# First expert's first weights in four buffers of later outputs, overflow loop ahead of group 3, low-part dispatch by token chunk

## The chip, the cores and the metric

The kernel runs on one core of a Trainium2 chip. The metric is the device time of one execution in microseconds (us); lower is better. Engines in the profile: PE is TensorE's matmuls and PEld its weight loads, DVE is VectorE, ACT is ScalarE, POOL is GpSimd, and SP is the queue of SyncE, on which all large loads are issued.

## The reference

One decoder block on 512 tokens of width 1024 in fp32. Two mixers work on the same normalized input, then a mixture of 32 experts with two experts for each token, then a small embedding term:

```python
u = rms_norm(h)
proj = u @ w_in
h = h + (sigmoid(gate_ssd) * ssd_branch(...) + sigmoid(gate_conv) * conformer_branch(...)) @ w_o
h = h + hier_moe(rms_norm(h))
h = h + (p @ w_ple_proj) * sigmoid(rms_norm(h) @ w_ple_gate)
out = rms_norm(h)

def hier_moe(u, wg, bg, we, be, w_gate, w_up, w_down):
    # top-1 of 4 groups, then the top-2 of its 8 experts, with softmax weights
    ...
    hdn = jax.nn.silu(xb @ w_gate[e]) * (xb @ w_up[e])     # 1024 x 512 each
    return hdn @ w_down[e]                                  # 512 x 1024
```

The weights of the 32 experts are 192 MB and all of them are read.

## The kernel before

The kernel is one stream of **units**. A unit has loads (one tile of weights each) and a function that makes its matmuls. `run(n)` calls `step()` until unit `n`; a step first calls `pump()`, then makes the unit's matmuls, then calls `free` for the pages that the unit has used, and runs the jobs and tasks that are due.

`pump()` (line 270) issues the loads in order on SP, as far as `state["room"]` allows. Room is counted in half pages: a raw load of the mixers (512 KB, tag "raw") takes one, a load of expert weights (1 MB, `wide`, tag "w") takes two. There are 11 pages of 1 MB under tag "w", one of which holds the one-hot matrices, so ten expert loads can be ahead of PE. The jobs `job(XD + 1, free, 2)` and the four of `job(NB - i, free, ...)` raise the room in the last mixer units, so that the first expert loads start before the experts do. All waits are set by the tile framework from the use of the tiles: a load into a page waits for the last matmul that read it.

The stages of the profiled execution: mixers and their output projection to about 530 us, the router and the one-hots to 550, experts to 1031, and the end stage (embedding term, norm, output) to 1102.

Of the experts, 7 **groups** are formed (`GROUPS`), each of one or two **quads** of two or three experts. A quad has four gate/up units (`gu_unit`: tensors eg and eu, the halves kp of the contraction) and two down units (`d_unit`: ed). Each of these units takes one load for each expert of its quad. A token's row is sent to its experts' slots by one-hot matmuls, `disp(gi, kp)`, four for a group and 16 matmuls each: eight with the high part `uh` and eight with the low part `ul`. The outputs `y` of a group's experts lie in the tiles ct, btok, k4 and bt and are brought back to the tokens by eight `combine`s, in group 2 of 4 matmuls each (tiles ct, btok, k, bt against glu). `disp`s of the next group and `combine`s of the last one are **tasks**: they are put between the units when a credit of PE time allows it.

The router's one-hots come last ahead of the experts; group 0's four dispatches are made by hand: all high-part matmuls, then (as `u2_lo` makes the low part, first all chunks c of half n = 0, then of half n = 1) the low-part ones, bank by bank.

An overflow loop, `with tc.For_i(0, n_ext)` (lines 1704 and 1705), serves tokens that do not fit their expert's slots. `n_ext` is read on the chip; with these inputs it is 0 and the loop's body is not run. In before it stands behind `run(NC)`, which is behind all experts and ahead of the end stage; SP has issued seven of the eight w_ple_gate loads of the end stage by then.

Of the kernel before, what the change touches and what calls it, by code (L numbers as in the profile page):

```python
# [19 lines left out]
NT = T // 128  # L20
# [47 lines left out]

_CST = {}
PAGES = 11  # L70
BT = dict(room=8, raw=20, hi=1, page=1.27, mm=3.5, cap=5.0, sp=5, fill=[1.8, 0.9], late=[7, 2])


# [63 lines left out]
def tile_hybrid(ctx: ExitStack, tc: tile.TileContext, x, p, chan, rowv, rows, cst, w_in, w_ssd, w_conf, w_o,  # L137
# [111 lines left out]
    jobs = defaultdict(list)  # L249
    state = {"pairs": 0, "n": 0, "load": 0, "room": 4, "split": 0, "lo": 0, "credit": 0, "top": 0}  # L250

    def load(src, wide):
        loads.append(dict(src=src, wide=wide))
        return loads[-1]

    def unit(src, mms, cost=0.0, plain=False):
        srcs = [] if src is None else src if isinstance(src, list) else [src]
        units.append(dict(lds=[load(s, plain) for s in srcs], mms=mms, cost=cost, plain=plain))
        return len(units) - 1

    def job(n, f, *a):
        jobs[n].append((f, a))
# [4 lines left out]
    def task(early, late, cost, f, *a):  # L267
        tasks.append((early, late, cost, f, a))

    def pump():  # L270
        while state["load"] < len(loads):
            ld = loads[state["load"]]
            if state["room"] <= (1 if ld["wide"] else 0):
                return
            src = ld["src"]()
            if ld["wide"]:
                state["room"] -= 2
                ld["t"] = st([128] + list(src.shape[1:]), F32, "w", PAGES)
            else:
                state["room"] -= 1  # L280
                ld["t"] = page([128] + list(src.shape[1:]), F32, "raw")
            nc.sync.dma_start(ld["t"], src)
            state["load"] += 1

    def free(n):
        state["room"] += n
# [68 lines left out]
    def step():  # L355
        n = state["n"]
        top = state["top"]
        if n < NB:
            while state["split"] <= min(max(n + 2, 2 * n - NB + BT["sp"]), top):
                split()  # L360
        else:
            while state["split"] <= min(top, n + (BT["hi"] if n < NC else 6)) and split_hi():
                split_lo()
        pump()
        u = units[n]
        if u["plain"]:
            ws = [ld["t"] for ld in u["lds"]]
            u["mms"](ws)
            free(2 * len(ws))
        elif u["mms"] is not None:  # L370
            u["mms"](u["wh"], u["wl"])
        after(u)

    def run(upto=None):
        while state["n"] < (len(units) if upto is None else upto):
            step()
# [529 lines left out]
    for c in range(NT):  # L906
        js.extend(chunk(c, f0 + c * TUNE["stride"]))
    XD = math.ceil(max(j[0] for j in js if j[1] in (ssd_diag, ssd_skip)))
    job(XD + 1, free, 2)
    if TUNE["first"]:  # L910
        step_jobs(js)
    for w in seq:
# [146 lines left out]
    job(NO, load_h)  # L1059
    NB = len(units)  # L1060
    for i in range(4, 0, -1):
        job(NB - i, free, 2 if i > 1 else BT["raw"] - BT["room"] - 8)

    def add_h(c, n):
        hv = hh_["h"][:, c, n * 512:(n + 1) * 512]
# [134 lines left out]
    def gu_unit(gi, q, i, kp):  # L1200
        quad = GROUPS[gi][q]

        def mms(ws):
            if kp == 0:
                PG[gi, q, i] = acc()
            for kk in range(4):
# [3 lines left out]
        return unit([lambda b=m[0]: weights((eg, eu)[i], b)[:, 4 * kp:4 * kp + 4, :] for m in quad], mms, BT["mm"],  # L1210
                    True)

    def d_unit(gi, q, fp):
        quad = GROUPS[gi][q]

        def mms(ws):
            if fp == 0:
                PY[gi, q] = [acc2(), acc2()]
            for f in (2 * fp, 2 * fp + 1):
                for n in range(2):  # L1220
                    strips(PY[gi, q][n], HT[gi, q][:, f, :], [w[:, f % 2, n * 512:(n + 1) * 512] for w in ws], quad,
                           f == 0, f == 3)
        return unit([lambda b=m[0]: weights(ed, b)[:, 2 * fp:2 * fp + 2, :] for m in quad], mms, BT["mm"], True)
# [112 lines left out]
        fill_pe(state["n"], room)  # L1336

    combined = NB + 4
    for gi, g in enumerate(GROUPS):
        last = gi == len(GROUPS) - 1  # L1340
        first = len(units)
        if last:
            for n in range(2):
                p_unit(n)
            job(first - 6, free, -2)
            job(first - 5, p_load)
            job(first - 5, free, -2)
            for k in range(2):
                job(first - 3 + k, p_tr, k)
            job(first - 2, free, 2)  # L1350
            job(first - 2, free, -8)
        for q in range(len(g)):
            for kp in range(2):
                for i in range(2):
                    u = gu_unit(gi, q, i, kp)
            job(u - 1, hid_act, gi, q)
            job(u, hid_mul, gi, q)
            job(u, fill_now, BT["fill"][0])
# [16 lines left out]
            continue  # L1375
        for n in range(2):
            for c in range(NT):
                task(u + 1, u + 5, 0.23 * 2 * len(g), combine, gi, c, n)
        combined = u + 5
        o = first + (BT["late"][0] if gi == 0 else BT["late"][1])  # L1380
        for q in range(len(GROUPS[gi + 1])):
            job(o, hot, gi + 1, q)
        for kp in range(4):
            task(o + 1, u, 0.115 * 16, disp, gi + 1, kp)
    for i in range(3):
        unit(None, None)
    NC = len(units)
# [201 lines left out]
    for c in range(NT):  # L1589
        hot_first(c)  # L1590
    for i in range(2 * NT):
        u2_lo(i // NT, i % NT)
    N2 = 2 * NEXP


# [93 lines left out]
    for i, f in enumerate((order0, order4, order1, order2, order3, order5, order6, order7, order8)):  # L1689
        job(NB + (i + 1) // 2, f)  # L1690
    pts = [acc() for _ in range(4)]
    for a in range(2):
        for k in range(4):
            disp_mm(0, k, pts[k], a)
    for k in range(4):
        disp_out(0, k, pts[k])
        if k % 2:
            step()
            step()
    run(NC)  # L1700

    W32 = [128, NEXP]
    ext, ntot, icnt, eidf, pos, gat = (R[n] for n in ("ext", "ntot", "icnt", "eidf", "pos", "gat"))
# [1 line left out]
    with tc.For_i(0, n_ext):  # L1705
# [120 lines left out]
                nc.vector.tensor_add(hv, hv, po)  # L1826
        nc.vector.tensor_scalar(icnt, icnt, 1.0, None, op0=OP.add)
    banks.remove(bank)
    if dbg == "moe":
        for c in range(NT):  # L1830
            nc.sync.dma_start(out[c * 128:(c + 1) * 128, :], h[:, c, :])
        return
# [77 lines left out]
```

## Time and profile before

| | us |
|---|---|
| median of 3 runs | 1103.64 |
| range of the runs | 1099.38 to 1104.58 |
| profiled execution, own time | 1103.84 |
| its span, first to last instruction | 1102.1 |
| PE matmuls busy | 1017.3 (92%) |
| VectorE busy | 561.7 (51%) |
| ScalarE busy | 344.7 (31%) |
| DMA traffic | 255.97 MB, 232 GB/s over the span |

The mean granted clock of TensorE is 0.978 of full speed. PE's share of busy time is an average over stages with different limits: what sets the pace is read stretch by stretch, from the DMA's rate and from what PE waits for. In the names, w is a page of weights, eg, eu and ed are the gate, up and down weights of the experts, cj the dispatched tokens, m the hidden activations, Z the residual stream, acc a bank of PSUM.

### The profile page before, as it was taken

How to read it: one execution, taken by the hardware profiler on the slowest of the kernel's cores; microseconds unless marked ns; L12 is line 12 of the kernel's file. 1: busy time of each engine (PE TensorE's matmuls, PEld its weight loads, DVE VectorE, ACT ScalarE, POOL GpSimd, SP SyncE). 2: the span in 40 equal slices, each digit the busy share in tenths (PEclk: the TensorE clock that was granted, in tenths of full speed). 3: DMA queues.
4: the chain of work that ended last, by engine and by line, in shares of the span. 5: the costliest groups of instructions: out<-in, count | busy, mean ns of one | idle time of the engine just before them, and what ended most of it. 6: DMA issues, size and time to landing. Idle time of an engine off the chain costs nothing. (4 is left out here: it accounts for less than half of the span.)

```text
span 1102.1 us, 15676 instructions
## 1 busy us (share of the span) xinstructions
PE 1017.3 (92%) x6262; PEld 673.0 (61%) x6262; DVE 561.7 (51%) x1004; ACT 344.7 (31%) x646; POOL 14.7 (1%) x32
## 2 busy tenths in 40 slices
PE   5999999999989999999799998989979979889796
PEld 4788889877767877788634453433514415345385
DVE  6689998897889955563721311202103002022365
ACT  5433446766443234432411010100100100121263
POOL 1000000000000000000000000000000000000010
PEclk9999999999999999999899999999999999999899
DMA  9323222201422323356189999999999999998701
GB/s 267 95 70 102 89 78 77 77 1 41 113 77 82 110 77 115 109 195 224 40 350 388 372 387 422 420 421 421 420 421 420 420 421 421 417 401 367 284 2 76
DMA packets 95660, 255.97 MB, mean 232 GB/s; under 512 B 4784, under 2 KB 62144, under 8 KB 71008
## 3 DMA queue, kind: packets, MB, share of 16 engines
q1 hardware_dynamic: 94896, 252.73, 60.6%
q0 software_dynamic: 688, 2.22, 0.7%
q8 instruction: 50, 0.82, 0.3%
q14 instruction: 26, 0.21, 0.1%
HBM read 252.83 MB, written 2.10 MB: 231 GB/s over the span
## 5 line engine op out<-in xcount | busy, mean ns | idle before, releaser
L120 PE MATMUL acc<-uh,w 128*128 128x512 f32 x704 | 231.0, 401 | 1.7 <-DVE w L120 1.6
L120 PE MATMUL acc<-w,cj 128*32 128x512 f32 x1664 | 200.3, 599 | 13.6 <-DMA w<-eu 9.9
L120 PE MATMUL acc<-w,uh 128*128 128x256 f32 (+2 forms) x752 | 161.7, 325 | 0.9 <-DVE w L120 0.9
L120 PEld LDWEIGHTS acc<-uh,w 128*128 128x128 f32 x704 | 132.2, 188 | 32.7 <-DVE w L120 2.6
L120 PE MATMUL acc<-w,m 128*32 128x512 f32 (+1 forms) x960 | 132.3, 595 | 19.2 <-DMA w<-ed 14.5
L120 PEld LDWEIGHTS acc<-w,cj 128*32 128x32 f32 x1664 | 54.4, 110 | 137.4 <-issue 106.6
L120 PE MATMUL acc<-ul,w 128*128 128x512 f32 x352 | 137.2, 390 | 0.0
L120 DVE SCALAR_TENSOR_TENSOR cj<-glu,chan,cj 128x512 f32<-128x512 f32 x180 | 130.8, 747 | 2.2
L120 PEld LDWEIGHTS acc<-w,uh 128*128 128x128 f32 x752 | 118.4, 193 | 21.0 <-issue 10.2
L120 DVE TENSOR_TENSOR w<-w 128x1024 fp32r<-128x1024 f32 x86 | 104.6, 1221 | 43.4 <-ACT w L302 43.2
L120 PE MATMUL acc<-w,ul 128*128 128x256 f32 (+2 forms) x488 | 117.2, 307 | 0.0
L302 ACT CAST w<-w 128x1024 fp32r<-128x1024 f32 x86 | 89.6, 1052 | 67.5 <-PE acc L120 54.4
L120 PE MATMUL acc<-w 128*128 128x512 f32 x384 | 102.0, 404 | 3.1 <-ACT w L302 2.4
L120 PEld LDWEIGHTS acc<-w,m 128*32 128x32 f32 (+1 forms) x960 | 44.5, 127 | 91.2 <-issue 53.1
L120 DVE TENSOR_TENSOR k<-k,acc 128x512 f32<-128x512 f32 x21 | 19.2, 913 | 151.4 <-PE acc L120 151.4
L120 PEld LDWEIGHTS acc<-w 128*128 128x128 f32 x384 | 73.9, 194 | 22.2 <-ACT w L302 2.8
L120 DVE TENSOR_TENSOR Z<-Z,acc 128x512 f32<-128x512 f32 x64 | 43.3, 686 | 85.1 <-PE acc L120 85.1
L120 PEld LDWEIGHTS acc<-w,ul 128*128 128x128 f32 x488 | 77.2, 189 | 5.6
L120 PEld LDWEIGHTS acc<-ul,w 128*128 128x128 f32 x352 | 66.2, 188 | 15.1 <-issue 1.7
L1227 ACT ACTIVATE k<-acc 128x512 f32<-128x512 f32 x13 | 7.8, 597 | 160.9 <-PE acc L120 160.9
L120 DVE SCALAR_TENSOR_TENSOR bt<-glu,chan,bt 128x512 f32<-128x512 f32 x60 | 43.0, 748 | 0.7
L120 DVE SCALAR_TENSOR_TENSOR bt<-acc,gt,k 128x512 fp32r<-128x512 f32 x12 | 9.0, 751 | 66.8 <-ACT k L1311 66.1
(270 smaller groups left out, 885.6 us busy)
## 6 DMA issues: line engine op xcount, KB each, us to landing
w<-eg SPq DMA_DIRECT2D x64, 1024.0 KB, 13.7
w<-eu SPq DMA_DIRECT2D x64, 1024.0 KB, 14.8
w<-ed SPq DMA_DIRECT2D x64, 1024.0 KB, 15.1
w<-w_in SPq DMA_DIRECT2D x52, 512.0 KB, 5.1
w<-w_ssd_out SPq DMA_DIRECT2D x8, 512.0 KB, 5.3
w<-w_conf_out SPq DMA_DIRECT2D x8, 512.0 KB, 4.3
w<-w_o SPq DMA_DIRECT2D x8, 512.0 KB, 4.8
w<-w_ple_gate SPq DMA_DIRECT2D x8, 512.0 KB, 13.3
```

The lines of the kernel that those rows point to most:

```text
L120: return f(*a, **k)
L302: nc.scalar.copy(u["wh"], u["raw"])
L1227: nc.scalar.activation(t, PG.pop((gi, q, 0)), AF.Silu)
```

## The change

There are four parts.

1. The first gate/up unit of group 0 becomes `first_unit`: its two loads of 1 MB become four of 512 KB, and these go to the tiles k4 (two buffers), ct and btok, which else are first written by the experts' outputs. Loads with a tag need no room and give none back.
2. The room that is given ahead of the experts comes later: the job behind the mixer's `ssd` steps goes, and the last of the four jobs gives 6 half pages in place of 4.
3. The overflow loop moves from behind the experts to the place between group 2 and group 3 (`LG = 3`). The eight combines of group 2 are made as jobs on its last down unit, ahead of the loop; the four dispatches of group 3, before tasks inside group 2, come right behind the loop.
4. The low part of the first dispatch is made by token chunk: `u2_lo` makes both halves of a chunk before the next, and the low-part matmuls run over the chunks outside and the eight column blocks inside, so that the four banks are complete together.

The loads on SP where the experts' first weights come, before:

```order
L282 DMA w<-w_o 128x2x512 x8
L282 DMA w<-eg 128x2048 x2
L1025 DMA Z<-x 128x1024 x4
L282 DMA w<-eu 128x2048 x2
L282 DMA w<-eg 128x2048 x2
L282 DMA w<-eu 128x2048 x2
```

and now:

```order
L287 DMA w<-w_o 128x2x512 x8
L287 DMA k_3754<-eg 128x1024
L287 DMA k_3756<-eg 128x1024
L287 DMA ct<-eg 128x1024
L287 DMA btok<-eg 128x1024
L287 DMA w<-eu 128x2048
L1029 DMA Z<-x 128x1024 x4
L287 DMA w<-eu 128x2048
```

The first unit's weights are out of the pages, and 1 MB of eu now stands ahead of the four loads of x.

On SP at the loop's new place, with what each row waits for (DMAHW are the counters of SP's loads, eight in all), now:

```order
L287 DMA w<-eg 128x2048 [waits DMAHW7_49,PE_49]
L287 ISA
L287 DMA w<-eu 128x2048 [waits DMAHW0_49,PE_49]
L1731 TENSOR_LOAD cd [waits DVE_49]
L1731 ISA x2
L1732 COMPARE_AND_BRANCH
L1732 UNCONDITIONAL_BRANCH [waits SP_sequencer_49,DMAHW0_49,DMAHW1_49,DMAHW2_49,DMAHW3_49,DMAHW4_49,DMAHW5_49,DMAHW6_49,DMAHW7_49]
```

These rows stood, in before, behind the loads of the end stage, without the waits:

```order
L282 DMA w<-ed 128x2048
L282 DMA w<-w_ple_gate 128x2x512 x7
L1704 TENSOR_LOAD cd
L1704 ISA x2
L1705 COMPARE_AND_BRANCH
L1705 UNCONDITIONAL_BRANCH x2
```

Seven loads of group 3 stand ahead of the loop on SP, and the eighth behind it.

On PE at the start of group 3, before (w,cj is a gate/up unit of 32 matmuls; ct, btok, k, bt against glu are one combine of group 2):

```order
L120 MATMUL acc<-bt,glu 128x512
L120 MATMUL acc<-w,cj 32x512 x16
L120 MATMUL acc<-ct,glu 128x512
L120 MATMUL acc<-btok,glu 128x512
L120 MATMUL acc<-k_5827,glu 128x512
L120 MATMUL acc<-bt,glu 128x512
L120 MATMUL acc<-ct,glu 128x512
L120 MATMUL acc<-btok,glu 128x512
L120 MATMUL acc<-k_5827,glu 128x512
L120 MATMUL acc<-bt,glu 128x512
L120 MATMUL acc<-w,cj 32x512 x32
L120 MATMUL acc<-w,uh 128x256 x8
```

and now, from the end of the loop (w,uh and w,ul are the two parts of a dispatch):

```order
L1732 REGISTER_ALU
L1732 COMPARE_AND_BRANCH
L1732 UNCONDITIONAL_BRANCH
L122 MATMUL acc<-w,uh 128x256 x8
L122 MATMUL acc<-w,ul 128x256 x8
L122 MATMUL acc<-w,uh 128x256 x8
L122 MATMUL acc<-w,ul 128x256 x8
L122 MATMUL acc<-w,uh 128x256 x8
L122 MATMUL acc<-w,ul 128x256 x8
L122 MATMUL acc<-w,uh 128x256 x8
L122 MATMUL acc<-w,ul 128x256 x8
L122 MATMUL acc<-w,cj 32x512 x64
```

All eight combines of group 2 are ahead of the loop; four dispatches of group 3 follow it, and only then the group's gate/up units, with no other work between them.

The diff:

```diff
--- before.py
+++ after.py
@@ -68,6 +68,8 @@
 
 _CST = {}
 PAGES = 11
+
+LG = 3
 BT = dict(room=8, raw=20, hi=1, page=1.27, mm=3.5, cap=5.0, sp=5, fill=[1.8, 0.9], late=[7, 2])
 
 
@@ -249,13 +251,14 @@
     jobs = defaultdict(list)
     state = {"pairs": 0, "n": 0, "load": 0, "room": 4, "split": 0, "lo": 0, "credit": 0, "top": 0}
 
-    def load(src, wide):
-        loads.append(dict(src=src, wide=wide))
+    def load(src, wide, tag=None):
+        loads.append(dict(src=src, wide=wide, tag=tag))
         return loads[-1]
 
-    def unit(src, mms, cost=0.0, plain=False):
+    def unit(src, mms, cost=0.0, plain=False, tags=None):
         srcs = [] if src is None else src if isinstance(src, list) else [src]
-        units.append(dict(lds=[load(s, plain) for s in srcs], mms=mms, cost=cost, plain=plain))
+        lds = [load(s, plain, t) for s, t in zip(srcs, tags or [None] * len(srcs))]
+        units.append(dict(lds=lds, mms=mms, cost=cost, plain=plain))
         return len(units) - 1
 
     def job(n, f, *a):
@@ -270,10 +273,12 @@
     def pump():
         while state["load"] < len(loads):
             ld = loads[state["load"]]
-            if state["room"] <= (1 if ld["wide"] else 0):
+            if not ld["tag"] and state["room"] <= (1 if ld["wide"] else 0):
                 return
             src = ld["src"]()
-            if ld["wide"]:
+            if ld["tag"]:
+                ld["t"] = st([128] + list(src.shape[1:]), F32, *ld["tag"])
+            elif ld["wide"]:
                 state["room"] -= 2
                 ld["t"] = st([128] + list(src.shape[1:]), F32, "w", PAGES)
             else:
@@ -366,7 +371,7 @@
         if u["plain"]:
             ws = [ld["t"] for ld in u["lds"]]
             u["mms"](ws)
-            free(2 * len(ws))
+            free(sum(2 for ld in u["lds"] if not ld["tag"]))
         elif u["mms"] is not None:
             u["mms"](u["wh"], u["wl"])
         after(u)
@@ -906,7 +911,6 @@
     for c in range(NT):
         js.extend(chunk(c, f0 + c * TUNE["stride"]))
     XD = math.ceil(max(j[0] for j in js if j[1] in (ssd_diag, ssd_skip)))
-    job(XD + 1, free, 2)
     if TUNE["first"]:
         step_jobs(js)
     for w in seq:
@@ -1059,7 +1063,7 @@
     job(NO, load_h)
     NB = len(units)
     for i in range(4, 0, -1):
-        job(NB - i, free, 2 if i > 1 else BT["raw"] - BT["room"] - 8)
+        job(NB - i, free, 2 if i > 1 else BT["raw"] - BT["room"] - 6)
 
     def add_h(c, n):
         hv = hh_["h"][:, c, n * 512:(n + 1) * 512]
@@ -1209,6 +1213,18 @@
                        k == 0, k == KD - 1)
         return unit([lambda b=m[0]: weights((eg, eu)[i], b)[:, 4 * kp:4 * kp + 4, :] for m in quad], mms, BT["mm"],
                     True)
+
+    def first_unit():
+
+        quad = GROUPS[0][0]
+
+        def mms(ws):
+            PG[0, 0, 0] = acc()
+            for k in range(4):
+                strips(PG[0, 0, 0], XT[0, k // 2][:, k % 2, :QS], [ws[2 * e + k // 2][:, k % 2, :] for e in range(2)],
+                       quad, k == 0, False)
+        return unit([lambda b=m[0], i=i: weights(eg, b)[:, 2 * i:2 * i + 2, :] for m in quad for i in range(2)], mms,
+                    BT["mm"], True, [("k4", 2), ("k4", 2), ("ct", 1), ("btok", 1)])
 
     def d_unit(gi, q, fp):
         quad = GROUPS[gi][q]
@@ -1336,9 +1352,12 @@
         fill_pe(state["n"], room)
 
     combined = NB + 4
+    NL = None
     for gi, g in enumerate(GROUPS):
         last = gi == len(GROUPS) - 1
         first = len(units)
+        if gi == LG:
+            NL = first
         if last:
             for n in range(2):
                 p_unit(n)
@@ -1352,7 +1371,7 @@
         for q in range(len(g)):
             for kp in range(2):
                 for i in range(2):
-                    u = gu_unit(gi, q, i, kp)
+                    u = first_unit() if gi == q == i == kp == 0 else gu_unit(gi, q, i, kp)
             job(u - 1, hid_act, gi, q)
             job(u, hid_mul, gi, q)
             job(u, fill_now, BT["fill"][0])
@@ -1375,13 +1394,17 @@
             continue
         for n in range(2):
             for c in range(NT):
+                if gi == LG - 1:
+                    job(u, combine, gi, c, n)
+                    continue
                 task(u + 1, u + 5, 0.23 * 2 * len(g), combine, gi, c, n)
         combined = u + 5
         o = first + (BT["late"][0] if gi == 0 else BT["late"][1])
         for q in range(len(GROUPS[gi + 1])):
             job(o, hot, gi + 1, q)
         for kp in range(4):
-            task(o + 1, u, 0.115 * 16, disp, gi + 1, kp)
+            if gi != LG - 1:
+                task(o + 1, u, 0.115 * 16, disp, gi + 1, kp)
     for i in range(3):
         unit(None, None)
     NC = len(units)
@@ -1589,7 +1612,7 @@
     for c in range(NT):
         hot_first(c)
     for i in range(2 * NT):
-        u2_lo(i // NT, i % NT)
+        u2_lo(i % 2, i // 2)
     N2 = 2 * NEXP
 
 
@@ -1689,15 +1712,19 @@
     for i, f in enumerate((order0, order4, order1, order2, order3, order5, order6, order7, order8)):
         job(NB + (i + 1) // 2, f)
     pts = [acc() for _ in range(4)]
-    for a in range(2):
-        for k in range(4):
-            disp_mm(0, k, pts[k], a)
+    for k in range(4):
+        disp_mm(0, k, pts[k], 0)
+    w = GW[0]
+    for c in range(NT):
+        for k in range(KD):
+            mm(pts[k // 2][:, k % 2 * w:(k % 2 + 1) * w], R["u2l"][:, c, k * 128:(k + 1) * 128], G["oh", 0][:, c, :w],
+               False, c == NT - 1 and k % 2 == 1)
     for k in range(4):
         disp_out(0, k, pts[k])
         if k % 2:
             step()
             step()
-    run(NC)
+    run(NL)
 
     W32 = [128, NEXP]
     ext, ntot, icnt, eidf, pos, gat = (R[n] for n in ("ext", "ntot", "icnt", "eidf", "pos", "gat"))
@@ -1826,6 +1853,9 @@
                 nc.vector.tensor_add(hv, hv, po)
         nc.vector.tensor_scalar(icnt, icnt, 1.0, None, op0=OP.add)
     banks.remove(bank)
+    for kp in range(4):
+        disp(LG, kp)
+    run(NC)
     if dbg == "moe":
         for c in range(NT):
             nc.sync.dma_start(out[c * 128:(c + 1) * 128, :], h[:, c, :])
```

## Rows read from the trace of the kernel before

**Rows 1.** The page, the span in 40 equal slices: the DMA's GB/s.
```profile
GB/s 267 95 70 102 89 78 77 77 1 41 113 77 82 110 77 115 109 195 224 40 350 388 372 387 422 420 421 421 420 421 420 420 421 421 417 401 367 284 2 76
```
**Rows 2.** Windows: busy us (instructions) of each engine in three stretches; columns above.
```profile
core 0: us, PE busy (x) PEld busy (x) DVE busy (x) ACT busy (x) POOL busy (x), PEclk, DMA share, GB/s
553.00:600.00 47.00, 45.04 (x388) 20.09 (x384) 9.39 (x39) 6.56 (x11) 0.00 (x0) 0.96 0.95 377
741.00:780.00 39.00, 35.65 (x250) 15.09 (x251) 9.52 (x16) 3.16 (x6) 0.00 (x0) 0.96 1.01 421
980.00:1000.00 20.00, 20.00 (x114) 11.79 (x110) 4.64 (x5) 7.28 (x12) 0.00 (x0) 0.96 0.82 319
```
**Rows 3.** PE's waits, largest of 533-660 and of 660-1031: total us, times, longest.
```profile
PE acc L120 <- DVE dtx L120: 5.6, 1, 5.6
...
PE acc L120 <- DMA w<-ed: 14.5, 13, 2.3
```
**Rows 4.** Timeline of SP, 525 to 660: start, length, loads issued.
```profile
528.79 25.39 SPq L282 DMA_DIRECT2D w<-ed  x3
...
580.42 4.25 SPq L282 DMA_DIRECT2D w<-ed  x4
```
**Rows 5.** Single loads issued at 580.42, 747.68 and 757.91: KB, us to landing.
```profile
w<-ed SPq DMA_DIRECT2D x1, 1024.0 KB, 5.0
...
w<-eu SPq DMA_DIRECT2D x1, 1024.0 KB, 19.8
...
w<-ed SPq DMA_DIRECT2D x1, 1024.0 KB, 19.4
```
**Rows 6.** Tile Z, 485 to 510: ns of one, first and last start.
```profile
L1025 SPq DMA_DIRECT2D Z<-x x4: 328/422/430, 486.7 to 488.0; - x4
...
L120 DVE TENSOR_TENSOR Z<-Z,acc x4: 687/687/687, 494.4 to 498.6; 128x512 f32<-128x512 f32 x4
```
**Rows 7.** Timelines of PE and of ACT in the router, 538 to 551.
```profile
545.99 3.79 PE L120 MATMUL acc<-w,ul 128*128 128x256 f32 x32
...
547.09 0.59 ACT L1278 COPY cj<-acc 128x512 f32<-128x512 f32 x1 [8.98 <-PE acc L120]
```
**Rows 8.** Timeline around the loop's place in before, 1028 to 1047.
```profile
1040.69 1.22 DVE L120 TENSOR_TENSOR w<-w 128x1024 fp32r<-128x1024 f32 x1
...
1042.42 3.15 PE L120 MATMUL acc<-ident,Z 128*128 128x128 f32 x16 [3.53 <-DVEq L1705]
...
1043.94 0.75 DVE L120 SCALAR_TENSOR_TENSOR ul<-acc,chan,uh 128x512 fp32r<-128x512 f32 x1 [2.03 <-PE acc L120]
...
1045.22 1.20 PE L120 MATMUL acc<-w,uh 128*128 128x512 f32 x2
```
**Rows 9.** Line 1705, the loop: ns min/median/max, first and last start in us.
```profile
L1705 SPq EVENT_SEMAPHORE  x21: 17/28/2061, 1029.3 to 1042.0; - x21
...
L1705 DVEq COMPARE_BRANCH  x3: 41/51/61, 1039.8 to 1043.7; - x3
```
**Rows 10.** Timeline of SP at the boundary of groups 2 and 3, 730 to 786.
```profile
747.68 6.96 SPq L282 DMA_DIRECT2D w<-eu  x2
```
**Rows 11.** Timeline of PE at the same place, 741 to 787.
```profile
750.09 4.56 PE L120 MATMUL acc<-w,m 128*32 128x512 f32 x25 [1.44 <-DMA w<-ed]
...
758.63 0.50 PE L120 MATMUL acc<-ct,glu 128*128 128x512 f32 x1
...
764.40 3.64 PE L120 MATMUL acc<-w,cj 128*32 128x512 f32 x32
...
777.03 1.18 PE L120 MATMUL acc<-w,uh 128*128 128x256 f32 x8
...
778.96 0.60 PE L120 MATMUL acc<-ident,k 128*128 128x128 f32 x4
```
**Rows 12.** Windows, one stretch behind PE's waits of 745 to 750 (columns as in rows 2).
```profile
749.50:752.90 3.40, 2.81 (x16) 0.79 (x20) 0.00 (x0) 0.00 (x0) 0.00 (x0) 0.50 1.02 424
```
**Rows 13.** Timeline of PE, 974 to 1030.
```profile
977.97 5.32 PE L120 MATMUL acc<-w,m 128*32 128x512 f32 x26 [2.29 <-DMA w<-ed]
```

## The prediction

> **What bounds the kernel now.** I read the page's slices first: their GB/s row swings between 1 and 390 until the 25th slice and then stands at 420 nearly to the end [rows 1]. Stretch by stretch the windows say the same: 553 to 600 us has TensorE's matmuls (PE) busy 45 of 47 us at 377 GB/s, so PE sets the pace there; from 741 to 780 the weights arrive at 421 GB/s and PE idles 3.4 of 39 us; from 980 to 1000 PE is busy all 20 us and the DMA falls to 319 GB/s [rows 2]. PE's waits agree. Between 533 and 660 us the largest is 5.6 us for VectorE in the router, and no wait for a load of weights is listed; between 660 and 1031 us its largest item is 14.5 us for ed loads [rows 3]. So from about 650 to 1031 us the stream of weights is the bound, 1 MB (1.049 million bytes at 420 GB/s) in 2.5 us, and what stops that stream for a microsecond costs one.
>
> **First weights.** In before, ten pages hold the first ten loads; the row of three ed issues from 528.79 lasts 25.39 us, since the third waits until the first expert unit gives pages back [rows 4]. With the first two loads in other buffers, the first twelve land before PE has finished a unit. The thirteenth still waits for the second unit's pages, as it does in before. PE waits for no load until after 660 us [rows 3], and at 580.42 one ed load is back in 5.0 us, alone on an empty queue: the DMA had run dry waiting for a page that PE held [rows 4, 5]. The lead is gone by then. I take 0. The bounds are 0 and a gain of two loads, 2 x 2.5 = 5.0 us, if the lead lasted into the stretch that the DMA bounds. The x loads into Z stand behind 1 MB more on SP, 2.5 us; they are issued from 486.7, and VectorE's first addition needs them at 494.4, 7.7 us later [rows 6]; 2.5 + 5.0 us for a load on an empty queue [rows 5] is 7.5. So 0, with 0.5 us at worst. The raw pages that come two later lie in a stretch where loads land tens of microseconds ahead of use: 0.
>
> **Router.** In before the low part is 32 matmuls from 545.99 to 549.7, and the first copy out of PSUM runs at 547.09, when the first quarter is finished, for 0.59 us [rows 7]; the first expert matmul follows the 32nd at once. The new order finishes all four banks only in its last eight matmuls, which begin at 549.7 - 0.9 = 548.8, so the first copy moves to about 549.1, ends at 549.7, and the first expert matmul moves to about 549.9: +0.2 us (0.1 to 0.6, where one copy shows in full).
>
> **The loop at the end, removed.** PE sits idle 3.53 us ahead of its transposes at 1042.42, released by VectorE's sequencer at the loop's line, and VectorE 2.03 us at 1043.94 [rows 8]. Without the loop the transposes follow the last combine directly, but VectorE is at a weight split until 1040.69 + 1.22 = 1041.9, and makes ul (0.75 us) before the first products. These come at 1045.22 now [rows 8]; 1041.9 + 0.75 + 0.1 = 1042.75 then, 2.5 us earlier. Since PE no longer idles ahead of them, its clock may stay up where it would else fall (below): I take -2.9 us (-2.0, VectorE's idle alone, to -3.5, all of PE's).
>
> **The loop in the middle, added.** The order shows what passing it needs: SP waits at the branch for all eight DMA semaphores, and then every engine for all others. Nothing runs through it. (The loop's body runs zero times with these inputs: no load in the trace is issued by its lines.) Its own instructions are cheap, 41 to 61 ns a branch on VectorE, while SP's semaphore waits there go up to 2061 ns [rows 9]. [...]
>
> Step one, the drain. SP has issued seven loads of group 3 when it comes to the loop, the last of them the eu of 747.68, which lands 19.8 us later, at 767.5 [rows 5, 10]. PE's last down unit of group 2 ends at 754.65. Eight combines are 32 matmuls; 24 take 758.63 to 764.40, so 32 take 7.7 us, and with some 2 us for the four outputs ahead of them PE is through by 764.3 [rows 11]. The loads end last. At the end of before 0.4 us lie between the loop's last wait (1042.0) and PE's first matmul [rows 8, 9]: PE restarts at 768.0 and SP issues at about 768.1. A load on an empty queue takes 5.0 us [rows 5], so the next one lands at 773.1 and not, as the stream would have it, at 767.5 + 2.5 = 770.0. The DMA has lost 3.1 us.
>
> Step two, the refill. Of ten pages seven are full, so SP may issue three, the last landing at 778.1. The fourth waits for pages of the group's first unit, and in front of that unit the change has put four dispatches, which before had been done during group 2. One is 16 matmuls, 1.93 us (777.03 to 778.96 [rows 11]), so four are 7.7 us. [...] A unit takes 3.6 us (764.40 to 768.0 [rows 11]). 768.0 + 7.7 + 1.7 + 3.6 = 781.0, and 5.0 later, at 786.0, the fourth load is there. In before it is an ed begun at 757.9 that takes 19.4 us, 777.3 [rows 5]. The stream is now 8.7 us late: 7.0 if the clock holds, 9.4 if the first unit too sees half of it.
>
> Step three. Units two to four give eight pages back in all by 791.8, eight loads that last to 786.0 + 7 x 2.5 = 803.5. The ninth needs a down unit, and four dispatches of group 4, which had stood between units, now stand ahead of it: 791.8 + 7.7 + 3.6 + 0.7 (transposes) = 803.8, and 5.0 to land is 808.8, against 806.0 in a stream without a gap. 2.8 us more (1.5 to 3.5). From there a quad's four units give pages faster than the DMA fills them. Sum 11.5 us (8.5 to 12.9).
>
> All of it reaches the end: PE waits for ed in before at 977.97 for 2.29 us [rows 13], after which it has no slack that could take it back; the PE-bound stretch from 980 moves along as a whole.
>
> [...]
>
> **Sum.** The profiled execution took 1103.84 us (span 1102.1), 0.2 above the median of 1103.64. 1103.84 + 0 + 0.2 - 2.9 + 11.5 = 1112.6 us.
>
> **Rivals.** *Only the drain counts*: the stream loses 3.1 us at the loop, but the dispatches behind it cost the DMA nothing, because more pages are free than I count or PE gets further ahead while group 2 lacks dispatches. 1103.84 + 0.2 - 2.9 + 3.1 = 1104.2. For it speaks that PE has 14.5 us of waits for ed loads alone to spend after 660 [rows 3]; against it that ten pages hold 25 us of stream, and PE alone gives them back. *The loop is nearly free*, by the mechanism that SP's wait ends with loads already queued behind it: 1103.84 + 0.2 - 2.9 = 1101.1. Against it stand the order's waits for every DMA semaphore. *Faster*: this, and the first weights' lead of 5.0 us lasts: 1096.1. It decides from the point where PE waits for a load within the first two groups, and the rows show none. *The dear loop*, on my own side: passing it costs 2 us more on each engine since VectorE's last branch there came only at 1043.7, 1.7 us behind SP's last wait at 1042.0 [rows 9]; were that so on PE and SP in the new place, it would give 1114.6 and, with the upper end of each step, 1117.
>
> **How the numbers follow.** A measurement of this kernel tells some 0.5%, 5.5 us, from no change. My forecast, with its own range of 1109 to 1116, gets 0.58 and the dear loop 0.07, both slower by over 0.5% (from 1109.2). Only the drain: 0.17; the nearly free loop: 0.07; both within. Faster: 0.11. The range reaches down to the free loop and up to the dear one, 1100 to 1117. Slower 0.64, same 0.25, faster 0.11.
>
> **What would show it.** In the profile after, the DMA's windows should show a gap of about 3 us near 768, a second of 5 to 6 us near 780 and a third near 806, at 420 GB/s between them; PE idle from about 764 to 768 and at 0.5 granted behind it; no PE wait for loads before 660; first products of the end stage 2.5 us closer to the last combine. Wrong would be a stream that runs through 768 without a gap, a queue that is full again before 780, or first experts' units that start earlier than 549.

## The result and the profile after

The changed kernel takes 1109.03 us (median of 5 runs, 1108.62 to 1111.48). Runs of the kernel before beside it bring that one to 1102.14 us (5 runs, 1099.38 to 1104.58). The ratio is 1.007 with a 95% interval of 1.0052 to 1.0088: slower by 0.7%, or 6.9 us. The profiled execution of the changed kernel took 1109.03 us, its span is 1107.3 us, 5.2 us longer than the span of before; the profiled execution of before lay 1.7 us above its median.

The page has the loss in one row, the DMA's GB/s in 40 slices, to be laid beside [rows 1]:

```profile
GB/s 266 99 70 106 79 85 69 77 1 55 98 58 96 78 113 114 164 246 199 31 381 396 369 405 421 421 421 302 318 408 421 421 421 420 415 419 376 331 1 76
```

Three slices behind the 27th, at 302, 318 and 408, had been at 420. The windows of 10 us from 760 on (us, busy us of each engine, PE's granted clock, DMA share, GB/s) cut this finer:

```profile
760.00:770.00 10.00, 4.97 (x23) 4.97 (x24) 1.50 (x5) 0.59 (x1) 0.00 (x0) 0.66 0.47 161
770.00:780.00 10.00, 10.00 (x95) 6.28 (x97) 0.00 (x0) 1.76 (x3) 0.00 (x0) 1.00 0.54 190
780.00:790.00 10.00, 10.00 (x95) 3.78 (x88) 1.09 (x1) 0.60 (x1) 0.00 (x0) 1.00 0.98 408
790.00:800.00 10.00, 10.00 (x91) 7.43 (x89) 0.00 (x0) 2.83 (x5) 0.00 (x0) 1.00 1.00 416
800.00:810.00 10.00, 10.00 (x92) 4.83 (x92) 2.65 (x10) 2.44 (x4) 0.00 (x0) 1.00 0.87 330
810.00:820.00 10.00, 8.76 (x74) 2.32 (x66) 0.00 (x0) 0.60 (x1) 0.00 (x0) 1.00 0.98 393
```

At 420 GB/s the six would add up to 2520, and they add up to 1898. The stream of weights lost 622 x 10 / 420 = 14.8 us. In 741 to 780 of before it had lost none [rows 2].

PE's timeline around the loop, columns as in [rows 11]:

```profile
745.68 5.32 PE L122 MATMUL acc<-w,m 128*32 128x512 f32 x26 [1.45 <-DMA w<-ed]
750.92 0.50 PE L122 MATMUL acc<-ct,glu 128*128 128x512 f32 x1
...
758.34 0.40 PE L122 MATMUL acc<-bt,glu 128*128 128x512 f32 x1
765.03 2.08 PE L122 MATMUL acc<-w,uh 128*128 128x256 f32 x8 [6.29 <-issue]
...
774.76 13.94 PE L122 MATMUL acc<-w,cj 128*32 128x512 f32 x128
788.64 1.21 PE L122 MATMUL acc<-w,uh 128*128 128x256 f32 x8
...
796.62 3.64 PE L122 MATMUL acc<-w,m 128*32 128x512 f32 x32
```

and SP's, with single loads from the narrow windows at 743.26, 764.76 and 778.43 below it (us to landing last):

```profile
743.26 21.84 SPq L287 DMA_DIRECT2D w<-eu  x2
765.32 13.97 SPq L287 DMA_DIRECT2D w<-ed  x4
781.87 3.77 SPq L287 DMA_DIRECT2D w<-eg  x3
...
800.29 5.35 SPq L287 DMA_DIRECT2D w<-eg  x3
```
```profile
w<-eu SPq DMA_DIRECT2D x1, 1024.0 KB, 19.7
...
w<-eu SPq DMA_DIRECT2D x1, 1024.0 KB, 5.0
...
w<-ed SPq DMA_DIRECT2D x1, 1024.0 KB, 5.0
```

This is the picture that was forecast. The seventh load, of 743.26, lands at 763.0; PE is idle for 6.3 us; SP issues again at 764.76, and the lone load lands 5.0 us later, at 769.8. PE then makes four dispatches, until 774.7, and a first unit. The load that waits for the unit's pages goes out at 778.43 and lands at 783.4. Four dispatches of group 4 stand between the units and the down unit of 796.62, and SP, which has issued a load at 789.30, issues none until 800.29.

What was not forecast stands in the first rows. The last down unit of group 2 ends at 751.0, not at 754.65 [rows 11], and the seventh load lands at 763.0, not at 767.5 [rows 5]. The changed kernel came to the loop 4.5 us early. Most of this arises in the mixers. The largest of PE's waits between 300 and 535 us (total us, times, longest), before and after:

```profile
PE acc L120 <- ACT k L929: 2.9, 1, 2.9
```
```profile
PE acc L122 <- DVE dtx L122: 5.6, 1, 5.6
PE acc L122 <- DVE w L122: 3.1, 3, 1.6
```

(The dtx wait is the router's; it is in both, at 538.42 before and at 533.61 after, and only the window's end keeps it out of the first list.) The 2.9 us for the squares of the LayerNorm (line 929) is gone after. Before, it stands at 413.78, and the stretch behind it ran at a granted clock of 0.51 (414.90 to 418.40), while the same work ran at 1.00 after:

```profile
413.78 1.05 PE L120 MATMUL acc<-ones,k 128*128 128x1 f32 x8 [2.93 <-ACT k L929]
```
```profile
414.90:418.40 3.50, 3.50 (x9) 2.72 (x9) 1.62 (x2) 1.11 (x2) 0.00 (x0) 0.51 0.00 0
```
```profile
410.50:415.00 4.50, 4.50 (x30) 4.01 (x30) 0.00 (x0) 1.12 (x2) 0.00 (x0) 1.00 0.73 233
```

2.9 us and half of 3.5 make 4.7, and the router's wait comes 4.8 us earlier, 533.61 in place of 538.42.

At the end the changed kernel goes straight on, with nothing between combine and transposes. PE's last wait for weights before, and then the same wait and PE's first products after, to be compared with [rows 8]:

```profile
1029.17 5.32 PE L120 MATMUL acc<-w,m 128*32 128x512 f32 x26 [1.52 <-DMA w<-ed]
```
```profile
1038.25 3.62 PE L122 MATMUL acc<-w,m 128*32 128x512 f32 x26 [1.47 <-DMA w<-ed]
...
1046.18 1.91 PE L122 MATMUL acc<-ident,Z 128*128 128x128 f32 x16
...
1047.84 0.47 PE L122 MATMUL acc<-w,uh 128*128 128x512 f32 x1
...
1049.36 0.50 PE L122 MATMUL acc<-w,uh 128*128 128x512 f32 x1 [1.04 <-DVE w L122]
...
1051.81 0.50 PE L122 MATMUL acc<-w,ul 128*128 128x512 f32 x1 [0.83 <-DVE ul L122]
```

PE's last wait for an ed load is at 1029.17 before and at 1038.25 after, 9.1 us later. The transposes are 3.8 us later than before, the first products 2.6, and after the waits for VectorE's splits the span ends 5.2 us later: 3.9 us come back at the end. Not all of this is the loop's: 1.7 us are the last down unit, whose 26 matmuls take 5.32 us at a mean granted clock of 0.67 before (1029.2 to 1034.4) and 3.62 us at 1.00 after (1038.3 to 1041.8). (They take 5.16 us in a run below that has no loop at all, so it is not the loop's absence behind them that makes them short.) That leaves 2.2 us. The account of the two traces is then -4.5 (mixers, as the stream sees it) + 14.8 (loop) - 1.2 (given back by the stream between 820 us and its end) - 3.9 (end) = 5.2 us. The 1.2 is what remains, not a row; it fits that from 980 to 1000, where PE was busy throughout in before, its stream ran at 319 GB/s [rows 2] and that of the changed kernel at 410: the late stream caught up there.

### The profile page after: what moved, and what is told of

Same layout as the page of the kernel before. It is cut to its first block, busy times and chain, and to the rows that moved or that the text cites. A ratio compares the mean times of both kernels' runs of the same rounds, so it can differ in the third digit from the quotient of the medians.

```text
span 1107.3 us, 15680 instructions
## 1 busy us (share of the span) xinstructions
PE 1012.1 (91%) x6262; PEld 670.6 (61%) x6262; DVE 561.3 (51%) x1004; ACT 344.7 (31%) x646; POOL 14.5 (1%) x32
## 5 line engine op out<-in xcount | busy, mean ns | idle before, releaser
L122 PE MATMUL acc<-w,cj 128*32 128x512 f32 x1632 | 194.4, 594 | 16.3 <-DMA w<-eu 10.4
L122 PE MATMUL acc<-w,m 128*32 128x512 f32 (+1 forms) x960 | 128.3, 574 | 23.7 <-DMA w<-ed 18.4
## 6 DMA issues: line engine op xcount, KB each, us to landing
w<-ed SPq DMA_DIRECT2D x64, 1024.0 KB, 14.3
```

Of the source, the lines that this page charges most:

```text
L122: return f(*a, **k)
```

## The experiments

Three theories stood after this. A: the later raw pages gave the mixers their 4.7 us, and the moved loop costs far more than the drain that one sees. B: the terms of the prediction as put. C: the first weights' lead made the 4 us.

**The four parts apart.** The loop moved alone (part 3 of the diff, nothing else of it):

```diff
...
-    run(NC)
+    run(NL)
...
+    for kp in range(4):
+        disp(LG, kp)
+    run(NC)
```

> Before with the loop move alone (part 3: loop, eight combines ahead of it, four dispatches of group 3 behind it). Theory A (the later raw pages gave the mixers 4.7 us, the moved loop costs the weight stream 14.5 us and gives 3.9 back at the end): mixers as in before, first expert matmul at 549.7, the stream some 14 to 15 us later behind the loop, the whole 10 to 11 us slower than before. Theory B (the prediction as put: the later raw pages are worth nothing, the loop costs 11.5 and gives 2.9): 8.6 us slower, as 1112 us. Theory C (the first weights' lead made the whole 4 us): as A.

Measured: 1115.04 us beside 1101.86 of before, ratio 1.0129 (1.0095 to 1.0162), 13 us slower. The mixers are as in before (first expert matmul at 548.4, the 2.9 us wait is there). The profiled span is 1111.2 us, 9.1 above that of before; the other three runs were slower than the profiled one. By the interval the move costs 10.5 to 17.9 us: A's 10 to 11 reaches its lower end, and B's 8.6 is too little.

Parts 1, 2 and 4 without part 3:

```diff
...
-    run(NL)
+    run(NC)
...
```

> The changed kernel with the loop, the combines and the dispatches of group 3 back in their old places (parts 1, 2 and 4 alone). Theory A: first expert matmul near 545.6 and 4 us faster than before, near 1099. Theory B: 0.2 us slower than before. Theory C: 4 us faster, but with the mixers' end where it was and the lead arising in group 0.

Measured: 1098.65 us, ratio 0.9964 (0.9947 to 0.9981), 3.2 us by the medians. A and C hold, B falls. Part 2 alone tells them apart:

```diff
-    job(XD + 1, free, 2)
...
-        job(NB - i, free, 2 if i > 1 else BT["raw"] - BT["room"] - 8)
+        job(NB - i, free, 2 if i > 1 else BT["raw"] - BT["room"] - 6)
```

> Before with the room given later alone (part 2: two half pages not at the mixer's ssd steps but with the last raise). Theory A: PE's wait of 2.9 us for the LayerNorm squares near 414 is gone with its half-clock stretch, first expert matmul at 545.0, 4.7 us faster than before. Theories B and C: PE's waits as in before, no change (within 0.5 us).

Measured: 1098.48 us, ratio 0.9961 (0.9945 to 0.9977), on the same chip as the run above. PE's wait of 2.9 us is gone, and the first expert matmul is at 545.72. Part 2 alone gives all that parts 1, 2 and 4 give together, so the first weights' four buffers are worth nothing that can be measured. (Part 1 alone, with the room of before, was not run.) C falls. And part 4:

```diff
-        u2_lo(i // NT, i % NT)
+        u2_lo(i % 2, i // 2)
...
-    for a in range(2):
-        for k in range(4):
-            disp_mm(0, k, pts[k], a)
+    for k in range(4):
+        disp_mm(0, k, pts[k], 0)
+    w = GW[0]
+    for c in range(NT):
+        for k in range(KD):
+            mm(pts[k // 2][:, k % 2 * w:(k % 2 + 1) * w], R["u2l"][:, c, k * 128:(k + 1) * 128], G["oh", 0][:, c, :w],
+               False, c == NT - 1 and k % 2 == 1)
```

> Before with the low-part dispatch by token chunk alone (part 4). Theory A, from the two traces: first expert matmul 0.6 us later than in before, 550.3. Theory B, from the prediction: 0.2 us later, 549.9. Either way no change that the time can tell.

Measured: 1101.61 us, ratio 0.9997 (0.9982 to 1.0013); first expert matmul at 549.28, 9.8 us behind the first high-part matmul, where before has 9.9. Neither theory's shift, of 0.6 or 0.2 us, is seen. The 0.6 to 0.7 us that the two traces show between these points belong to a longer stretch at a granted clock of 0.50, from 535.0 to 541 after and from 539.8 to 544 before (the high part takes 6.99 us after and 6.36 before, and 7.07 in the run of part 2 alone), not to the order.

**Why half pages given later help.** In the order (the instructions of an engine with what each waits for, as shown under the change), the casts of the mixers' last weights wait in turn for VectorE and for PE in before, and each for both in the changed kernel. That is one reading of the gain. The rival is that the number of half pages counts. One half page in place of two:

```diff
-    job(XD + 1, free, 2)
+    job(XD + 1, free, 1)
...
-        job(NB - i, free, 2 if i > 1 else BT["raw"] - BT["room"] - 8)
+        job(NB - i, free, 2 if i > 1 else BT["raw"] - BT["room"] - 7)
```

> Before with one half page, not two, given later (one at the ssd steps as now, one with the last raise). In the order, the casts of the weights then wait in turn for VectorE and for PE, as in before, and not each for both, as in the changed kernel. Theory A (what counts is which page a cast falls on): PE's wait of 2.9 us near 414 stays and the time does not change (within 1 us). Rival (what counts is how much is given later): half the gain of e3_room_only, 2 us faster.

Measured: 1097.03 us, ratio 0.9941 (0.9917 to 0.9964). Both expectations failed: neither no change nor half the gain, but all of it. So the alternation of the casts as a whole isn't the cause. ScalarE's timeline shows which cast it is; before, and then this run:

```profile
404.41 0.63 ACT L929 ACTIVATE k<-bt 128x512 f32<-128x512 f32 x1 [0.32 <-ACT k L929]
410.10 1.04 ACT L302 CAST w<-w 128x1024 fp32r<-128x1024 f32 x1 [5.06 <-PE acc L120]
413.10 0.63 ACT L929 ACTIVATE k<-cj 128x512 f32<-128x512 f32 x1 [1.95 <-DVE cj L120]
```
```profile
402.86 0.63 ACT L929 ACTIVATE k<-bt 128x512 f32<-128x512 f32 x1 [0.32 <-ACT k L929]
403.40 1.04 ACT L302 CAST w<-w 128x1024 fp32r<-128x1024 f32 x1
406.41 0.63 ACT L929 ACTIVATE k<-cj 128x512 f32<-128x512 f32 x1 [1.97 <-DVE cj L120]
409.90 1.05 ACT L302 CAST w<-w 128x1024 fp32r<-128x1024 f32 x1 [2.85 <-PE acc L120]
```

One cast, of weights that are needed much later, is queued on ScalarE between the squares of the LayerNorm. Its page is the next in the ring of eleven. In before PE was still reading that page, so the cast waited 5.06 us. VectorE's subtraction for the same weights waited for the cast, the LayerNorm's next centred row stood behind the subtraction, and its square, which PE waits for, behind that row. The subtraction, before:

```profile
411.17 1.23 DVE L120 TENSOR_TENSOR w<-w 128x1024 fp32r<-128x1024 f32 x1 [7.16 <-ACT w L302]
```

With one or two half pages of raw weights fewer in flight the same cast finds a page that is free, and in the order it has lost its wait for PE:

```
L302 CAST w<-w 128x1024 [waits DMAHW7_49,PE_49]
```
```
L302 CAST w<-w 128x1024 [waits DMAHW7_49]
```

The first is before, the second this run; the run of part 2 alone has the second too. The casts of this run still wait in turn, as in before, but shifted by one: the cast between the squares is without a wait for PE, and the next one has it (2.85 us at 409.90), where PE loses nothing by it. The chain of waits is read from the traces; no run moved this cast alone. By the ratio, the kernel with one half page is the fastest of all that were run, faster than both kernels of the study. Against part 2 alone (0.9961) its interval overlaps, and which of the two is better stays open.

**The price of the loop at its old place.** Before without the loop:

```diff
-    n_ext = nc.values_load(ntot, min_val=0, max_val=T * 2 // SL + NEXP)
-    with tc.For_i(0, n_ext):
...
-    banks.remove(bank)
```

> Before without the overflow loop at all (left out: what would serve overflowing tokens, none with these inputs). It prices the loop at the end. Theory A (the changed kernel's stretch from the last load to the end): 3.9 us faster than before. Theory B (the prediction's term): 2.9 us faster. Rival: VectorE's work behind the combines hides the loop, under 1 us.

Measured: 1101.72 us beside 1102.32, ratio 0.9988 (0.9970 to 1.0005): A's 3.9 us falls, and B's 2.9 us, the rival's under 1 us and no change at all lie within the interval. The profiled span is 2.0 us shorter. The first products of the end stage come at 1040.20 and not at 1045.22 [rows 8], 5.0 us earlier, and 3.0 us of that are lost again:

```profile
1040.20 0.48 PE L120 MATMUL acc<-w,uh 128*128 128x512 f32 x1
...
1041.77 0.50 PE L120 MATMUL acc<-w,uh 128*128 128x512 f32 x1 [1.09 <-DVE w L120]
...
1044.23 0.50 PE L120 MATMUL acc<-w,ul 128*128 128x512 f32 x1 [0.83 <-DVE ul L120]
```

VectorE splits weights and makes ul for the same products. While PE stood at the loop, VectorE ran ahead; without the loop PE waits for it.

**What the moved loop costs, taken apart.** The changed kernel without the loop, with its order of combines and dispatches:

> The changed kernel without the overflow loop, with its PE order kept (eight combines of group 2, then four dispatches of group 3 ahead of its first unit; left out: the loop). Theory A (drain and order each cost; worked out by the prediction's steps two and three without the drain): PE is through the dispatches by 766 and the first unit by 770, so the stream loses about 2 us there and 3 us at group 4's dispatches, 5 of the 14.5; with 4.4 us from the mixers and 3.9 from the end the whole is near 1099, 3 us faster than before. Theory D (the drain alone is the price, the order is free): no gap of the stream near 770 to 810, 8 us faster than before. Theory O (the order is the price): the stream still loses 9 us, 1 us slower than before.

Measured: 1099.54 us, ratio 0.9968 (0.9949 to 0.9986), where A had 1099. D's 8 us faster and O's 1 us slower lie outside the interval. The windows of the same stretch:

```profile
760.00:770.00 10.00, 10.00 (x94) 5.57 (x96) 0.00 (x0) 1.76 (x3) 0.00 (x0) 1.00 0.87 334
770.00:780.00 10.00, 10.00 (x93) 4.49 (x85) 1.10 (x1) 0.82 (x2) 0.00 (x0) 1.00 1.01 424
780.00:790.00 10.00, 10.00 (x90) 7.24 (x88) 0.00 (x0) 2.77 (x6) 0.00 (x0) 1.00 0.92 380
790.00:800.00 10.00, 10.00 (x94) 4.32 (x98) 2.65 (x10) 2.28 (x4) 0.00 (x0) 1.00 0.98 375
800.00:810.00 10.00, 8.56 (x78) 2.40 (x74) 0.00 (x0) 0.60 (x1) 0.00 (x0) 1.00 1.01 401
```

At 420 GB/s the five would add up to 2100; they are short of it by 186, which is 4.4 us of stream, where A had 5. The order alone costs a third of 14.8 us, the loop with this order the rest.

The drain alone: before with a second loop at the same place, its body one instruction, and combines and dispatches as they were:

```diff
...
+    run(NL)
...
+    with tc.For_i(0, n_ext0):
+        nc.vector.memset(icnt0, 0.0)
     run(NC)
```

> Before with a second loop between groups 2 and 3, whose body is one instruction of VectorE and runs zero times; combines and dispatches stay as in before. It prices the drain alone. Theory A: the stream loses 4 to 5.5 us (the first lone load and the one behind it) and then runs on, as the first unit follows the loop at once: 4 to 5.5 us slower than before. Theory D (the drain with what it does to the pages is the whole price): 14 us slower. Theory F (passing a loop is nearly free): under 1 us.

Measured: 1111.86 us, ratio 1.0076 (1.0053 to 1.0100), 8.4 us slower by the ratio. A fell here: the drain without any dispatch behind it is not a matter of 4 to 5.5 us. D's 14 us is outside as well. PE's timeline shows what A had left out:

```profile
751.75 3.62 PE L120 MATMUL acc<-w,m 128*32 128x512 f32 x26 [1.44 <-DMA w<-ed]
769.65 5.84 PE L120 MATMUL acc<-w,cj 128*32 128x512 f32 x32 [14.29 <-DMA w<-eu]
...
781.20 3.64 PE L120 MATMUL acc<-w,cj 128*32 128x512 f32 x32
```

PE stands for 14.3 us, since the eight combines that fill 7.8 us of this time in the changed kernel now lie behind the loop, six between the first unit and the second (781.20) and two behind the second. The first unit itself takes 5.84 us in place of 3.64 [rows 11], at a mean granted clock of 0.57 from 769 to 775. The stream restarts (the four ed issues begin at 770.15), and then waits for PE's pages again (the next issues begin at 784.87): its windows from 755 to 821 are short of 420 GB/s by 11.6 us of stream. Together with the 4.4 us of the order alone that is 16.0, and the changed kernel has 14.8, so the two do not simply add up. Of the 11.6 us some 8.4 reach the time.

**Whether each gap counts.** If the stream's gaps were prices of their own, then moving dispatches from ahead of the first unit would pay. Two of the four dispatches behind the second unit:

```diff
-    for kp in range(4):
-        disp(LG, kp)
+    for kp in range(2):
+        disp(LG, kp)
+    for kp in range(2, 4):
+        job(NL + 1, disp, LG, kp)
```

> The changed kernel with two of group 3's four dispatches ahead of its first unit and two behind its second unit. Theory P (what counts is when PE, as a whole behind, gives back the pages of the down unit; the gaps ahead of it only share that delay out): first unit 3.9 us earlier and the second gap of the stream down from 5.2 to 1.5 us, but a new gap behind the second unit, and the stream after 806 as late as in the changed kernel; the time within 1 us of the changed kernel's 7 us over before. Theory G (each gap of the stream counts for itself, as the prediction's steps add them): 3.9 us faster than the changed kernel, 3 us over before.

Measured: 1109.30 us beside 1102.31, ratio 1.0067 (1.0046 to 1.0088): as slow as the changed kernel. Then the same with the planner's credit charged for the four dispatches, so that one dispatch of group 4 fewer stands ahead of the down unit:

```diff
+    state["credit"] -= 0.115 * 16 * 4
```

> e9_split_dispatch with the credit of PE time charged for the four dispatches, so that three and not four of group 4's dispatches stand ahead of group 3's first down unit. Theory P: one dispatch of 1.9 us fewer ahead of the down unit, the stream after 806 us 1.9 us earlier than in e9 and 5 us over before. Theory G: 1.9 us less again, 1 us over before. If the refill has nothing to do with it: no change, 7 us over before in both.

Measured: 1107.83 us, ratio 1.0046 (1.0031 to 1.0061). Both times are as theory P had them; the 95% intervals of the two runs overlap, but all five runs of the second are faster than all four of the first. The windows, of the first and then of the second:

```profile
770.00:780.00 10.00, 10.00 (x90) 4.85 (x89) 0.00 (x0) 0.73 (x2) 0.00 (x0) 1.00 0.86 333
...
790.00:800.00 10.00, 10.00 (x91) 7.36 (x89) 0.00 (x0) 2.83 (x5) 0.00 (x0) 1.00 0.71 297
```
```profile
770.00:780.00 10.00, 10.00 (x92) 5.44 (x88) 0.00 (x0) 1.13 (x2) 0.00 (x0) 1.00 0.96 378
...
790.00:800.00 10.00, 10.00 (x91) 5.56 (x94) 0.62 (x4) 1.76 (x3) 0.00 (x0) 1.00 0.73 279
```

In the first the window of 770 to 780 has gained 143 GB/s over the changed kernel, and the one of 790 to 800 has lost 119; from 760 to 820 its stream is short by 15.1 us, the changed kernel's by 14.8. The loads come earlier, run out earlier, and wait for the same down unit, whose matmuls begin at 796.55, in the changed kernel at 796.62. In the second they begin at 792.53, 4.0 us earlier than in the first, where P had 1.9: the dispatch that is gone makes 1.9 of it, 1.0 is that PE leaves the loop earlier (763.12 for 764.17), and 1.1 that its first two dispatches behind it take 5.4 us (763.12 to 768.50) and not 6.5 (764.17 to 770.66), at a mean granted clock of 0.69 against 0.66 from 760 to 770. So the second run doesn't price the dispatch alone.

## Why the prediction was right, and where it was not

The time (1109.0 for a forecast of 1112.6, at the lower edge of the range of 1109 to 1116) and the side were right, and the reason for the loss too: the stream of weights is drained at the loop, and PE, behind by the dispatches, refills it late. Term by term:

| term | forecast, us | measured, us (from the traces where nothing else is said) |
|---|---|---|
| first weights, x loads | 0 | 0 (parts 1, 2 and 4 beside part 2 alone) |
| later raw pages | 0 | -4.8 |
| router | +0.2 | 0 (its own run) |
| loop in the middle | +11.5 (8.5 to 12.9) | +14.8, of which 1.2 given back |
| loop gone from the end | -2.9 (-2.0 to -3.5) | -3.9 here, 1.7 of it the last down unit's clock; -2.0 where the loop was left out of before |

- **First weights: right.** PE waits for no load before 660 us in the changed kernel either, and parts 1, 2 and 4 together gain no more than part 2 alone.
- **Raw pages: the step that failed.** "The raw pages that come two later lie in a stretch where loads land tens of microseconds ahead of use: 0." The loads were not late. What it left out is that a raw load also takes a place in the ring of pages, so that every later tile of the ring falls on another page with another last reader. One cast between the LayerNorm's squares got rid of its wait, and PE of 2.9 us and a stretch of 3.5 us at 0.51 granted. One of the prediction's own signs of being wrong came with it, first experts' units that start earlier than 549: in the changed kernel the first starts at 545.60. No bound of this term reached below zero in the forecast, and the rivals had no such mechanism. PE's wait at 413.78 could be followed back in the trace of before, over ScalarE, VectorE and the cast, to PE itself.
- **Router: right in effect.** The later first copy is not seen in the time.
- **The loop in the middle: mechanism right, size short by 3.3 us.** The drain was put at 3.1; from the landing at 763.0 to the next at 769.8 it is 6.8 - 2.5 = 4.3, since SP takes 1.8 us from the last landing to the next issue, and not 0.6. The second load behind the loop lands 3.5 and not 2.5 us after the first. The second gap was put at 5.6 and is 7.7 - 2.5 = 5.2 (775.7 to 783.4). The rest of the 14.8, in landings behind 790, was put at 2.8 and is some 4.3. The sum of step two also has 1.7 us for PE's clock, a term that no run shows at the loop: there the four dispatches took 9.7 us (765.03 to 774.76) where 7.7 had been put, 2.0 us more, with 0.51 granted from 766 to 770. The dear loop, a rival, had a slow restart on every engine, at 2 us; SP was 1.2 us slower than forecast. "All of it reaches the end" was wrong by the 1.2 us that the stream gives back, and by more in the run with the empty loop.
- **The frame of steps one to three was wrong, though their sum was near.** The runs with split dispatches show that the gaps aren't prices that add up: filling the second made the third wider by as much. What fits both runs is that the time goes by when PE, late by its idle time at the loop (6.3 us in the changed kernel), the stretch at 0.51 granted and the dispatches, comes to the down unit that gives the next pages back.
- **The end: mechanism right, size within a microsecond.** "VectorE is at a weight split" was the right bound, but for later products than forecast. The first products begin 1.5 us behind the end of the last combine, in before 6.3 us: 4.8 us closer, and not 2.5. It is the products behind them that wait for the splits: PE's head start of 5.0 us where the loop was left out of before shrinks to 2.0. By its time, that run can't be told from no change. Without the last down unit's clock the term is -2.2 between the two traces, so the loop's own part lies at the small end of the range. The clock did stay up, as forecast: 16 transposes take 1.91 us after, at a granted clock of 1.00 (1046.2 to 1048.1), and 3.15 before, at a mean of 0.59 (1042.4 to 1045.6).

The errors had opposite signs: -4.5 for the raw pages as the stream sees them, -0.2 for the router, +3.3 for the loop, -1.2 given back and -1.0 at the end make the 3.6 us by which the time lies below the forecast. That it lies in the range is in part luck: with the raw pages as they came and all else as forecast it would have been 1108.1, below it.

## What to carry to other kernels

The loop that every engine must pass was a drain here (PE idle for 6.3 us): before one is put in a stretch that the DMA bounds, count what PE must do behind it until the next page comes free, not the gap that the queue shows; in this kernel it was dear there (13 us where it was moved alone) and cheap at the seam ahead of the end stage (0.6 us by the medians, 3.3 at the end of the interval), where the next work waited for VectorE as well. In a ring of buffers shared by loads and intermediate tiles, a change of how many loads are in flight moves every later tile to another buffer, so follow each wait of the engine that bounds back to the tile whose buffer it waits for, even if the load itself is early. And where a gap ahead of a bottleneck is closed, look at the next release before the gain is counted.

## What the runs showed of the hardware

Line 1732 in the changed kernel, the loop (ns min/median/max, first and last start in us), beside [rows 9]:

```profile
L1732 SPq EVENT_SEMAPHORE  x20: 17/28/28, 744.4 to 764.4; - x20
...
L1732 PEldq COMPARE_BRANCH  x3: 101/193/4561, 755.1 to 764.8; - x3
```

The seven loads have landed by 763.0, but SP's last semaphore step at the loop begins at 764.4, and one of PE's three branches lasts 4.56 us. In the 1.8 us between the landing and SP's next issue (764.76) the trace has one packet of an instruction queue, of 0.02 MB, and no load. In the run whose loop has a body of one instruction PE's longest branch takes 0.19 us, and in before, where the long body is passed over at the loop's old place, 0.33 us. What makes the restart slow is not shown. The stretch at a low clock behind the idling came as forecast: 6.3 us of idle PE, and then a granted clock of 0.51 from 766 to 770. A wait's length alone does not tell in these traces what the clock does: ahead of the last down unit PE waits for 1.32 and 1.52 us before and for 1.33 and 1.47 us after, and the mean granted clock in the unit is 0.67 before (1029.2 to 1034.4) and 1.00 after (1038.3 to 1041.8).

```profile
766.00:770.00 4.00, 4.00 (x21) 4.00 (x20) 0.00 (x0) 0.59 (x1) 0.00 (x0) 0.51 0.84 326
```
